# Starting every large on-chip tile of an encoder kernel at a multiple of 128 bytes

## The chip, the cores and the metric

The kernel runs on one core of a Trainium2 chip. The core has a matrix engine (TensorE, PE in the profile; its weight loads are listed apart as PEld), VectorE (DVE), ScalarE (ACT), GpSimd (POOL) and the engine that issues most transfers (SyncE, SP). They work side by side and wait for each other through semaphores. On-chip memory (SBUF) has 128 partitions; a tile takes the same stretch of bytes in each of them, and "place" below means the byte at which that stretch starts. The metric is the time of one execution in microseconds (us), lower is better.

## The reference

A two-layer encoder over 256 tokens of width 1024, float32:

```python
for i in range(2):
    hn = rms_norm(h, mix_norm[i])
    h = h + (retention_mixer(hn, ...) if i == 0 else fourier_mixer(hn, ...))
    hn = rms_norm(h, ffn_norm[i])
    h = h + (swiglu(hn, dense...) if i == 0 else moe_swiglu(hn, ...))   # 8 experts, top 2
return rms_norm(h, final_norm)

def swiglu(t, w_gate, w_up, w_down):
    return (jax.nn.silu(t @ w_gate) * (t @ w_up)) @ w_down
```

The retention mixer is four projections, rotary turns, a masked score product per head and an output product. The Fourier mixer is two small transform products and an output product. The expert layer (MoE) has 8 experts with a hidden width of 3584, so nearly all weights, and nearly all of the time, are there.

## The kernel before

Every large product is done in three matmuls per block, because each float32 operand is split in two rounded parts: `hi` and `lo = x - hi`. The weights come from memory in pieces of 1 MB (tile `raw`, issued by SP, up to 11 and for a while 15 buffers). ScalarE rounds a piece into `whi` (L103), VectorE subtracts it into `wlo` (L104), and TensorE uses the two parts. `whi` and `wlo` have three buffers each, in a pool of their own (`hilo`). The three matmuls are written in one helper, whose line numbers the profile shows:

```python
def mm3(o, lh, ll, rh, rl, first, last):
    te.matmul(o, lh, rh, start=first, stop=False)   # L225
    te.matmul(o, lh, rl, start=False, stop=False)   # L226
    te.matmul(o, ll, rh, start=False, stop=last)    # L227
```

The first operand (`lh` or `ll`, 128 columns of 4 bytes, so 512 bytes in a partition) is loaded into the array by a weight load, LDWEIGHTS in PEld. The second (`rh` or `rl`, 512 columns, so 2048 bytes) then streams through it. The profile writes a matmul as output<-streamed,loaded: `mm<-whi,xe` streams a piece of the weights through a loaded block of `xe`. So the model's weights are what streams, and the activations are what is loaded: every matmul loads another block of 512 bytes.

The loaded tiles by stage, in order of time:

- Retention (0 to about 230 us): `nhi`, `nlo` (the normalised input, transposed) for the projections; tiles named `th` (transposed queries, keys and gated outputs) for the scores and the output product; `ah`, `al` for the product of scores and values, where `vh`, `vl` stream.
- Dense layer (to about 402 us): `nhi`, `nlo` again, and `hth`, `htl` (the transposed hidden block) for the down product.
- Fourier stage (to about 450 us): `tsh`, `tsl` and `fh`, `fl` stream, `nhi` and `tdh`, `tdl` are loaded; then `yh`, `yl` are loaded for the output product.
- MoE (to the end): 56 units (8 experts by 7 blocks) of 48 matmuls that load `xe` and 24 that load `hth`, `htl`, with four transposes of the hidden block `hm` in each unit. For the last unit the transposed block is called `ht` and lies where `nhi` and `nlo` lay.

Order and waits come from the program text: `manual_schedule` keeps each engine's instructions as written. The places come from the tile pools. A pool lays its tiles one behind the other in the order in which their names first occur, each rounded up to 32 bytes, and a pool opened inside another begins behind it. Two small tiles of 32 bytes, `neg` and `iota8`, stand early in the pool `const`, so that all that follows in `const` starts 64 bytes past a multiple of 128. The pools of the stages (`pa`, `pb`, `pc`, `pe`, and `pt` at the right end) have such small tiles too.

Of the kernel before, what the change touches and what calls it, by code (L numbers as in the profile page):

```python
# [9 lines left out]
DT = mybir.dt  # L10
F32, F32R, BF, I32, U32 = DT.float32, DT.float32r, DT.bfloat16, DT.int32, DT.uint32
AF = mybir.ActivationFunctionType
OP = mybir.AluOpType
PS = bass.MemoryType.PSUM

P = 128
# [5 lines left out]
NE = 8  # L22
# [4 lines left out]
def cp(c):  # L27
    return slice(c * P, (c + 1) * P)
# [7 lines left out]
def cols(w, c0, n, k0, nk):  # L36

    return w.rearrange("(k p) n -> p k n", p=P)[:, k0:k0 + nk, c0:c0 + n]


class Weights:
# [82 lines left out]

def body(nc, tc, a, out, upto=None):
    with ExitStack() as ctx:
        const = ctx.enter_context(tc.tile_pool(name="const", bufs=1))
        r1 = ctx.enter_context(tc.tile_pool(name="r1", bufs=4))
        hilo = ctx.enter_context(tc.tile_pool(name="hilo", bufs=Weights.PARTS))
        ps = ctx.enter_context(tc.tile_pool(name="ps", bufs=1, space=PS))  # L130
# [66 lines left out]
        W.open(r1, 3, bufs=4)  # L197
        ident = const.tile([P, P], F32, name="ident")
        make_identity(nc, ident)
        neg = const.tile([P, 2], F32, name="neg")  # L200
        ge.memset(neg, -0.5)
        iota8 = const.tile([P, NE], F32, name="iota8")
        slot = const.tile([P, P], F32, name="slot")
        ones = const.tile([P, P], F32, name="ones")

        def route_consts(rw, upper):
            nc.scalar.dma_start(rw, a["moe_router"][0].rearrange("(k p) e -> p k e", p=P))
            kw = dict(base=0, allow_small_or_imprecise_dtypes=True)
            ge.iota(iota8, pattern=[[1, NE]], channel_multiplier=0, **kw)
            ge.iota(slot, pattern=[[1, P]], channel_multiplier=0, **kw)  # L210
            ge.memset(ones, 1.0)
            ge.iota(upper, pattern=[[1, P]], channel_multiplier=-1, **kw)
            ge.tensor_scalar(upper, upper, 0.0, None, op0=OP.is_gt)

        def acc(i):
            return ps.tile([P, 512], F32, name=f"acc{i}", tag=f"acc{i}")
# [32 lines left out]
        def scratch(pool):  # L249

            scr[:] = [pool.tile([P, 512], BF, name="scr")]
# [22 lines left out]
        def norm_tiles(pat, **kw):  # L274

            return [const.tile([P, 2048], F32R, name=n).rearrange(pat, **kw) for n in ("nhi", "nlo")]
# [43 lines left out]


        xh, xl = norm_tiles("p (k t) -> p k t", k=8)
        with tc.tile_pool(name="pa", bufs=1) as pa:
            scratch(pa)
            lx = pa.tile([P, 8], F32, name="lx")
            nc.scalar.dma_start(lx, bcast_rows(a["ret_decay_logit"][0], 8))
# [247 lines left out]

        H1 = P + 1
        pt_ = ctx.enter_context(ExitStack())
        pt = pt_.enter_context(tc.tile_pool(name="pt", bufs=1, side="right"))
        td = [pt.tile([P, 2, 512], F32R, name=n) for n in ("tdh", "tdl")]
        ts_ = [pt.tile([P, 2, 2 * H1], F32R, name=n) for n in ("tsh", "tsl")]
        rw = pt.tile([P, 8, NE], F32, name="rw")  # L580
        upper = pt.tile([P, P], F32, name="upper")
        with tc.tile_pool(name="pb", bufs=1) as pb:
            scratch(pb)
            tabr = pb.tile([P, 2, 2 * H1], F32, name="tabr")
            tabd = pb.tile([P, 2, 512], F32, name="tabd", tag="hth", bufs=2)
            accs = [acc(i) for i in range(4)]
            rst, sq = [], sq_tile()

            def dense_h(u, hooks={}):

                n, ns = (512, 2) if u < 5 else (256, 1)
                kn = 8 // ns
                o = []
                for s in range(ns):
                    wh, wl = W.get()
                    for c in range(2):
                        if not s:
                            o.append(mm())
                        for k in range(kn):
                            mm3(o[c][:, :n], xh[:, kn * s + k, cp(c)], xl[:, kn * s + k, cp(c)], wh[:, k], wl[:, k],  # L600
                                s == 0 and k == 0, s == ns - 1 and k == kn - 1)
                        run(hooks, 2 * s + c)
                return [x[:, :n] for x in o]

            def hidden(u):

                n = 4 if u < 5 else 2
                hT[u] = [pb.tile([P, 4, S], F32R, name=nm, bufs=2) for nm in ("hth", "htl")]
                return [lambda c=c: t4(hms[u][c], *(t[:, :n, cp(c)] for t in hT[u]), n) for c in range(2)]

            hms, hT = {}, {}
            for u in range(6):
                if u:
                    f = hidden(u - 1)
                    hooks = {0: f[:1], 1: f[1:]}
                else:
                    hooks = {1: [left]}
                n = 512 if u < 5 else 256
                g = dense_h(u, hooks)
                if not u:  # L620
                    for c in range(2):
                        for hf in range(2):
                            square(sq, c, hf)
                    rst = [inv_rms(sq, c) for c in range(2)]
                    nc.scalar.dma_start(tabr, a["dft_s"].rearrange("(c p) n -> p c n", p=P))
                    nc.scalar.dma_start(tabd, a["dft_d"].rearrange("(c p) n -> p c n", p=P))
                    gain_bcast(a["mix_norm"][1])
                    route_consts(rw, upper)
                gs = []
                for c in range(2):  # L630
                    t = pb.tile([P, 512], F32, name="gs", bufs=3)
                    se.activation(t[:, :n], g[c], AF.Silu, scale=rst[c])
                    gs.append(t)
                o = dense_h(u)
                if u == 1:
                    split(td[0], td[1], tabd)
                hms[u] = []
                for c in range(2):
                    t = pb.tile([P, 512], F32, name="hm", bufs=3)
                    ve.scalar_tensor_tensor(t[:, :n], o[c], rst[c], gs[c][:, :n], op0=OP.mult, op1=OP.mult)  # L640
                    hms[u].append(t)
                if 1 <= u < 5:
                    for s in range(2):
                        it = W.get()
                        for c in range(2):
                            out_mm(accs, it, *lhs(hT[u - 1], s), c, u == 1 and s == 0, False)
            it, f = W.get(), hidden(5)
            for c in range(2):
                out_mm(accs, it, *lhs(hT[4], 0), c, False, False)
                f[c]()  # L650
            its = [(W.get(), *lhs(hT[4], 1)), (W.get(hold=1), *lhs(hT[5], 0))]
            nh, nl = norm_tiles("p (c d) -> p c d", c=2)
            sq = sq_tile()

            rst = []

            def n_early(c, hf):
                square(sq, c, hf)
                if hf:
                    rst.append(inv_rms(sq, c))  # L660

            def n_sink(c, hf, xg):
                split(nh[:, c, HALF[hf]], nl[:, c, HALF[hf]], xg)
                if hf:
                    split_s(ts_[0][:, c], ts_[1][:, c], tabr[:, c], rst[c])
            left = close(its, accs, n_sink, n_early)
            left()
# [3 lines left out]


        with tc.tile_pool(name="pc", bufs=1) as pc:
            scratch(pc)
            gain_bcast(a["ffn_norm"][1])
            fq, yt = {}, {}
# [5 lines left out]
            def s1_out(o, g, b):  # L682

                if g % 2 == 0 and b == 0:
                    fq[g // 2] = [pc.tile([P, 2, 2, 2, H1], F32R, name=n, bufs=2) for n in ("fh", "fl")]
                h, l = fq[g // 2]
                split(h[:, b, :, g % 2], l[:, b, :, g % 2], o[:, :2 * H1].rearrange("p (w s) -> p w s", w=2))
# [28 lines left out]
            for c in range(2):  # L716
                for o, (g, b) in zip(early, gb8):
                    s1_mm(o, g, b, c)
                    if c:
                        s1_out(o, g, b)  # L720
            for p in range(2):
                stage2(p)
            accs = [acc(i) for i in range(4)]
# [80 lines left out]


        with tc.tile_pool(name="pe", bufs=1) as pe:
            def choose(e0):

                pm = pe.tile([P, 2, 2 * P], F32R, name="pm")
                for c in range(2):  # L810
                    for j in range(2):
                        ve.tensor_scalar(pm[:, c, cp(j)], slot, pos[:, c, e0 + j:e0 + j + 1],
                                         mask[:, c, e0 + j:e0 + j + 1], op0=OP.is_equal, op1=OP.mult)
                return pm
# [271 lines left out]
            for c in range(2):  # L1086
                x = [X[:, c, HALF[hf]] for hf in range(2)]
                se.activation(x[0], x[0], AF.Copy, scale=rs[c])  # L1088
                nc.scalar.dma_start(out[0, cp(c), HALF[0]], x[0])
                ve.scalar_tensor_tensor(x[1], of[c][1], rs[c], gb[:, HALF[1]], op0=OP.mult, op1=OP.mult)  # L1090
                nc.sync.dma_start(out[0, cp(c), HALF[1]], x[1])


NAMES = ["x", "mix_norm", "ffn_norm", "ret_w_in", "ret_decay_logit", "ret_gn_gain", "ret_w_out",
# [43 lines left out]
```

## Time and profile before

| | |
|---|---|
| median of 3 runs | 1451.75 us (1451.16 to 1452.35) |
| the profiled execution | 1451.45 us |
| its span, first to last instruction | 1449.6 us |
| PE busy in the span | 1430.3 us (99%) |
| DVE, ACT, POOL busy | 1184.3, 970.3, 61.5 us (82%, 67%, 4%) |
| granted TensorE clock, mean | 0.996 of full speed |
| moved by transfers | 431.70 MB, 298 GB/s on average |

A matmul's listed duration overlaps the next one's, so durations of one engine do not add up to its time. What adds up is the distance from one matmul's start to the next one's start, which is called the pace below.

### The profile page before, as it was taken

Reading aid. Unit: us, or ns where it says so; the run is one execution under the profiler, and the core shown is the slowest. Engines: PE = TensorE matmul, PEld = TensorE weight load, DVE = VectorE, ACT = ScalarE, POOL = GpSimd, SP = SyncE. Lnnn points to the kernel's source line nnn. Section 1 sums busy time; section 2 is a strip of 40 time slices with the busy share of each in tenths; the row PEclk is TensorE's granted clock in tenths of the full one; section 3 lists DMA queues with packets and bytes.
Section 4 is the critical chain, followed back from the end, with each engine's and each line's share of the span. In section 5 each row is a group of like instructions: output and inputs, shape, how many; then the busy total and the mean of one; then the engine's idle time right before and its main releaser. Section 6 shows DMA issues by size and latency. Waiting matters only on the chain. (4 is left out here: it accounts for less than half of the span.)

```text
span 1449.6 us, 17454 instructions
## 1 busy us (share of the span) xinstructions
PE 1430.3 (99%) x6603; PEld 1177.6 (81%) x6603; DVE 1184.3 (82%) x1236; ACT 970.3 (67%) x1123; POOL 61.5 (4%) x95
## 2 busy tenths in 40 slices
PE   8999999999999999999999999999999999999997
PEld 6888878888888888888888888888878888888886
DVE  6866666554577999989999998998989899999996
ACT  5544445443455777777877777777777777777875
POOL 8400000000001000000000000000000000000000
PEclk9999999999999999999999999999999999999999
DMA  7645549755526989999999999999999999999980
GB/s 285 211 151 200 170 139 362 247 183 175 198 103 239 382 311 362 348 336 345 347 357 372 376 348 334 368 365 352 338 388 341 342 360 379 352 378 375 348 317 29
DMA packets 185101, 431.70 MB, mean 298 GB/s; under 512 B 7977, under 2 KB 10801, under 8 KB 185010
## 3 DMA queue, kind: packets, MB, share of 16 engines
q1 hardware_dynamic: 181424, 426.27, 81.7%
q10 hardware_dynamic: 3586, 4.24, 0.9%
q8 instruction: 54, 0.88, 0.2%
q14 instruction: 37, 0.30, 0.1%
HBM read 429.44 MB, written 1.05 MB: 297 GB/s over the span
## 5 line engine op out<-in xcount | busy, mean ns | idle before, releaser
L104 DVE TENSOR_TENSOR wlo<-raw,whi 128x1024 fp32r<-128x1024 f32 (+1 forms) x789 | 923.4, 1218 | 146.4 <-ACT whi L103 140.4
L103 ACT CAST whi<-raw 128x1024 fp32r<-128x1024 f32 (+1 forms) x789 | 785.6, 1046 | 206.9 <-PE acc L227 105.7
L225 PE MATMUL mm<-whi,xe 128*128 128x512 f32 x896 | 355.3, 397 | 0.3 <-PEq L1064 0.3
L227 PE MATMUL mm<-whi,xe 128*128 128x512 f32 x896 | 350.0, 391 | 0.0
L226 PE MATMUL mm<-wlo,xe 128*128 128x512 f32 x896 | 349.1, 390 | 0.0
L226 PE MATMUL acc<-wlo,hth 128*128 128x512 f32 x528 | 208.2, 394 | 0.0
L225 PE MATMUL acc<-whi,hth 128*128 128x512 f32 x528 | 207.6, 393 | 0.0
L227 PE MATMUL acc<-whi,htl 128*128 128x512 f32 x528 | 205.6, 389 | 0.0
L227 PEld LDWEIGHTS mm<-whi,xe 128*128 128x128 f32 x896 | 168.2, 188 | 36.3
L225 PEld LDWEIGHTS mm<-whi,xe 128*128 128x128 f32 x896 | 168.3, 188 | 35.1 <-issue 2.2
L226 PEld LDWEIGHTS mm<-wlo,xe 128*128 128x128 f32 x896 | 168.5, 188 | 32.9
L225 PE MATMUL mm<-whi,nhi 128*128 128x512 f32 (+1 forms) x352 | 137.2, 390 | 0.0
L226 PE MATMUL mm<-wlo,nhi 128*128 128x512 f32 (+1 forms) x352 | 135.3, 384 | 0.0
L227 PE MATMUL mm<-whi,nlo 128*128 128x512 f32 (+1 forms) x352 | 135.3, 384 | 0.0
L225 PEld LDWEIGHTS acc<-whi,hth 128*128 128x128 f32 x528 | 99.1, 188 | 22.9
L227 PEld LDWEIGHTS acc<-whi,htl 128*128 128x128 f32 x528 | 99.1, 188 | 22.5
L226 PEld LDWEIGHTS acc<-wlo,hth 128*128 128x128 f32 x528 | 99.3, 188 | 20.2
L230 ACT CAST hth<-tr 128x512 fp32r<-128x512 f32 (+1 forms) x67 | 38.9, 581 | 91.1 <-PE tr L271 91.1
L227 PEld LDWEIGHTS mm<-whi,nlo 128*128 128x128 f32 x352 | 66.2, 188 | 14.6
L226 PEld LDWEIGHTS mm<-wlo,nhi 128*128 128x128 f32 x352 | 66.2, 188 | 13.5
L225 PEld LDWEIGHTS mm<-whi,nhi 128*128 128x128 f32 x352 | 66.2, 188 | 13.5
L231 DVE TENSOR_TENSOR htl<-tr,hth 128x512 fp32r<-128x512 f32 (+1 forms) x67 | 45.7, 681 | 33.8 <-ACT hth L230 33.7
(279 smaller groups left out, 1038.7 us busy)
## 6 DMA issues: line engine op xcount, KB each, us to landing
raw<-in_moe_w_gate SPq DMA_DIRECT2D x110, 1024.0 KB, 7.0
raw<-in_moe_w_down SPq DMA_DIRECT2D x108, 1024.0 KB, 7.1
raw<-in_moe_w_up SPq DMA_DIRECT2D x105, 1024.0 KB, 6.9
raw<-in_ret_w_in SPq DMA_DIRECT2D x23, 1024.0 KB, 5.2
raw<-in_dense_w_gate SPq DMA_DIRECT2D x11, 1024.0 KB, 5.2
raw<-in_dense_w_up SPq DMA_DIRECT2D x11, 1024.0 KB, 8.6
raw<-in_dense_w_down SPq DMA_DIRECT2D x11, 1024.0 KB, 5.4
raw<-in_ret_w_out SPq DMA_DIRECT2D x8, 1024.0 KB, 4.8
```

The source lines that it names most:

```text
L103: self.nc.scalar.copy(hi[sl], t[sl])
L104: self.nc.vector.tensor_sub(lo[sl], t[sl], hi[sl].bitcast(F32))
L225: te.matmul(o, lh, rh, start=first, stop=False)
L226: te.matmul(o, lh, rl, start=False, stop=False)
L227: te.matmul(o, ll, rh, start=False, stop=last)
L230: se.copy(hi, src)
L231: ve.tensor_sub(lo, src, hi.bitcast(F32))
```

## The change

A class `Aligned` is put around the pools `const`, `pa`, `pb`, `pc`, `pe` and `pt`. When a name occurs for the first time and its tile has 512 bytes or more in a partition, the class first takes a gap tile that nothing uses, so that the tile starts at a multiple of 128 bytes. `neg` and `iota8` move behind `nhi` and `nlo`. `upper` loses its own tile: it takes that of `tsh` after the first transform product, and is made there instead of in `route_consts`. No instruction is added or taken away, and no shape changes.

```diff
+class Aligned:
+    ALIGN = 128
+    def tile(self, shape, dtype, name, tag=None, bufs=1):
+        kw = dict(name=name, bufs=bufs, **({"tag": tag} if tag else {}))
+        size = math.prod(shape[1:]) * DT.size(dtype)
+        key = tag or name
+        if key not in self.seen:
+            self.seen.add(key)
+            gap = -self.at % self.ALIGN if size >= 512 else 0
+            if gap:
+                self.pool.tile([P, gap // 4], F32, name=f"gap{len(self.seen)}")
+            self.at += gap + bufs * (-(-size // 32) * 32)
+        return self.pool.tile(shape, dtype, **kw)
...
-        const = ctx.enter_context(tc.tile_pool(name="const", bufs=1))
+        const = Aligned(ctx.enter_context(tc.tile_pool(name="const", bufs=1)))
...
-        neg = const.tile([P, 2], F32, name="neg")
-        ge.memset(neg, -0.5)
-        iota8 = const.tile([P, NE], F32, name="iota8")
...
         xh, xl = norm_tiles("p (k t) -> p k t", k=8)
+        neg = const.tile([P, 2], F32, name="neg")
+        ge.memset(neg, -0.5)
+        iota8 = const.tile([P, NE], F32, name="iota8")
...
-        upper = pt.tile([P, P], F32, name="upper")
+        pt.fill(96)
...
-            ge.iota(upper, pattern=[[1, P]], channel_multiplier=-1, **kw)
-            ge.tensor_scalar(upper, upper, 0.0, None, op0=OP.is_gt)
...
+            upper = pt.tile([P, P], F32, name="upper", tag="tsh")
+            ge.iota(upper, pattern=[[1, P]], base=0, channel_multiplier=-1, allow_small_or_imprecise_dtypes=True)
+            ge.tensor_scalar(upper, upper, 0.0, None, op0=OP.is_gt)
             for p in range(2):
                 stage2(p)
```

Where the tiles lie in the two built programs, as the remainder of their place by 128, 256 and 512 (all slices of these tiles that a matmul loads or streams start at multiples of 512 bytes inside the tile, so they share these remainders; `whi`, `wlo`, `raw`, `xe`, `pm`, `y`, the placing tile `pt` of the MoE and `X` are where they were):

| tile | before: 128, 256, 512 | after: 128, 256, 512 |
|---|---|---|
| `whi`, `wlo` (streamed) | 0, 128, 128 | the same |
| `xe` | 0, 128, 128 | the same |
| `nhi`, `nlo`, `ht` | 64, 192, 192 | 0, 128, 128 |
| `th` of queries and keys, and of heads 1 and 3 | 96, 96, 352 | 0, 128, 128 |
| `th` of heads 0 and 2 | 32, 32, 32 | 0, 128, 384 |
| `ah`, `al` (with `vh`, `vl` streamed) | 64, 192, 192 (96, 96, 352) | 0, 128, 384 (0, 128, 128) |
| `hth`, `htl` of the dense layer | 32, 160, 160 | 0, 0, 256 |
| `yh`, `yl` | 0, 0, 256 | 0, 128, 384 |
| `hth`, `htl` of the MoE | 64, 64, 320 | 0, 128, 384 |
| `hm` of the MoE | 64, 64, 320 | 0, 128, 384 |

Only POOL's order changes. Its instructions from the end of the retention stage to the routing stage, before: `rs` is an inverse root of a norm, `slot`, `ones` and `upper` are constants of the routing, `w` are the routing weights.

```order
L264 TENSOR_TENSOR rs<-rs,neg 128x1 x2
L209 IOTA iota_90 128x8
L210 IOTA slot 128x128
L211 MEMSET ones 128x128
L212 IOTA upper 128x128
L213 TENSOR_SCALAR upper<-upper 128x128
L264 TENSOR_TENSOR rs<-rs,neg 128x1 x2
L759 MEMSET w 128x2
L760 TENSOR_TENSOR w<-sq 128x2
```

The same stretch of POOL after the change:

```order
L286 TENSOR_TENSOR rs<-rs,neg 128x1 x2
L233 IOTA iota_94 128x8
L234 IOTA slot 128x128
L235 MEMSET ones 128x128
L286 TENSOR_TENSOR rs<-rs,neg 128x1 x2
L750 IOTA upper 128x128
L751 TENSOR_SCALAR upper<-upper 128x128
L790 MEMSET w 128x2
L791 TENSOR_TENSOR w<-sq 128x2
```

The two instructions that make `upper` have moved behind the two roots of the dense layer's end; the first of them now waits for the matmuls that read `tsh`. The rows of the other engines are the same in both programs but for line and buffer numbers.

## Rows read from the trace of the kernel before

**Rows 1.** The page, busy time of each engine (us, share of the span, instructions).
```profile
PE 1430.3 (99%) x6603; PEld 1177.6 (81%) x6603; DVE 1184.3 (82%) x1236; ACT 970.3 (67%) x1123; POOL 61.5 (4%) x95
```

**Rows 2.** Waits of PE, first and last of nine: us, times, longest us.
```profile
PE tr L375 <- DMA X<-in_x: 2.3, 1, 2.3
...
PE mm L225 <- PEq L1064: 0.3, 1, 0.3
```

**Rows 3.** Busy time by window; the column names are the first line.
```profile
core 0: us, PE busy (x) PEld busy (x) DVE busy (x) ACT busy (x) POOL busy (x), PEclk, DMA share, GB/s
450.00:1400.00 950.00, 947.41 (x4335) 782.97 (x4335) 867.03 (x849) 727.65 (x798) 5.21 (x17) 1.00 0.98 356
```

**Rows 4.** Groups of PE instructions, MoE (470 to 1449 us): busy us, mean ns.
```profile
L226 PE MATMUL mm<-wlo,xe 128*128 128x512 f32 x883 | 344.0, 390 | 0.0
...
L226 PE MATMUL acc<-wlo,hth 128*128 128x512 f32 x440 | 173.4, 394 | 0.0
```

**Rows 5.** The same view before the MoE (0 to 450 us).
```profile
L226 PE MATMUL mm<-wlo,nhi 128*128 128x512 f32 x320 | 126.4, 395 | 0.0
...
L226 PE MATMUL acc<-wlo,hth 128*128 128x512 f32 x88 | 34.8, 396 | 0.0
...
L226 PE MATMUL acc<-wlo,th 128*128 128x512 f32 x64 | 25.3, 395 | 0.0
...
L226 PE MATMUL acc<-wlo,yh 128*128 128x512 f32 x32 | 12.6, 395 | 0.0
```

**Rows 6.** Timeline of PE (start us, duration us), `xe`, 21 matmuls apart.
```profile
898.40 0.39 PE L225 MATMUL mm<-whi,xe 128*128 128x512 f32 x1
...
903.16 0.39 PE L225 MATMUL mm<-whi,xe 128*128 128x512 f32 x1
```

**Rows 7.** Timeline of PE, `hth` of the MoE, 18 matmuls apart.
```profile
903.84 0.39 PE L225 MATMUL acc<-whi,hth 128*128 128x512 f32 x1
...
907.96 0.39 PE L225 MATMUL acc<-whi,hth 128*128 128x512 f32 x1
```

**Rows 8.** Timeline of PE, `ht` of the last unit, 18 matmuls apart.
```profile
1434.70 0.39 PE L225 MATMUL acc<-whi,ht 128*128 128x512 f32 x1
...
1438.90 0.39 PE L225 MATMUL acc<-whi,ht 128*128 128x512 f32 x1
```

**Rows 9.** Timeline of PE, `nhi` in the retention stage, 60 matmuls apart.
```profile
60.41 0.40 PE L225 MATMUL mm<-whi,nhi 128*128 128x512 f32 x1
...
74.41 0.40 PE L225 MATMUL mm<-whi,nhi 128*128 128x512 f32 x1
```

**Rows 10.** Timeline of PE, `yh` in the Fourier stage, 21 matmuls apart.
```profile
430.63 0.39 PE L226 MATMUL acc<-wlo,yh 128*128 128x512 f32 x1
...
435.53 0.40 PE L226 MATMUL acc<-wlo,yh 128*128 128x512 f32 x1
```

**Rows 11.** Groups of weight loads, whole run: busy us, mean ns, idle before.
```profile
L226 PEld LDWEIGHTS mm<-wlo,xe 128*128 128x128 f32 x896 | 168.5, 188 | 32.9
...
L226 PEld LDWEIGHTS mm<-wlo,nhi 128*128 128x128 f32 x352 | 66.2, 188 | 13.5
```

**Rows 12.** Chain that ended last (start us, us): transposes of two units in a row.
```profile
1177.74 0.44 PE tr L271 x4
...
1194.61 0.44 PE tr L271 x4
```

**Rows 13.** Timeline of PE behind a unit's transposes, 11 matmuls apart.
```profile
1419.01 0.40 PE L226 MATMUL mm<-wlo,xe 128*128 128x512 f32 x1
...
1421.55 0.39 PE L225 MATMUL mm<-whi,xe 128*128 128x512 f32 x1
```

**Rows 14.** Waits of ACT (us, times, longest), and transfers (KB, us to landing).
```profile
ACT whi L103 <- PE acc L227: 110.1, 105, 3.6
...
raw<-in_moe_w_gate SPq DMA_DIRECT2D x110, 1024.0 KB, 7.0
```

**Rows 15.** Timelines of POOL and PE: `upper` is finished, and first read.
```profile
231.58 0.55 POOL L213 TENSOR_SCALAR upper<-upper 128x128 f32<-128x128 f32 x1
...
450.14 0.37 PE L793 MATMUL po<-mask,upper 128*128 128x8 f32 x2
```

More of the change, by code (lines that the diff above doesn't have):

```diff
@@ L38, in cols, with __init__, fill @@
     return w.rearrange("(k p) n -> p k n", p=P)[:, k0:k0 + nk, c0:c0 + n]
+class Aligned:
+    ALIGN = 128
+    def __init__(self, pool):
+        self.pool, self.at, self.seen = pool, 0, set()
+    def tile(self, shape, dtype, name, tag=None, bufs=1):
[9 more added lines that the diff above has]
+        return self.pool.tile(shape, dtype, **kw)
+    def fill(self, over=0):
+        gap = (over - self.at) % self.ALIGN
+        if gap:
+            self.pool.tile([P, gap // 4], F32, name="gap")
 class Weights:
@@ L199, in body, with route_consts @@
         make_identity(nc, ident)
-        neg = const.tile([P, 2], F32, name="neg")
-        ge.memset(neg, -0.5)
-        iota8 = const.tile([P, NE], F32, name="iota8")
         slot = const.tile([P, P], F32, name="slot")
         ones = const.tile([P, P], F32, name="ones")
-        def route_consts(rw, upper):
+        def route_consts(rw):
             nc.scalar.dma_start(rw, a["moe_router"][0].rearrange("(k p) e -> p k e", p=P))
@@ L322, in body @@
         xh, xl = norm_tiles("p (k t) -> p k t", k=8)
+        neg = const.tile([P, 2], F32, name="neg")
+        ge.memset(neg, -0.5)
+        iota8 = const.tile([P, NE], F32, name="iota8")
         with tc.tile_pool(name="pa", bufs=1) as pa:
+            pa = Aligned(pa)
             scratch(pa)
@@ L576, in body @@
         pt_ = ctx.enter_context(ExitStack())
-        pt = pt_.enter_context(tc.tile_pool(name="pt", bufs=1, side="right"))
+        pt = Aligned(pt_.enter_context(tc.tile_pool(name="pt", bufs=1, side="right")))
         td = [pt.tile([P, 2, 512], F32R, name=n) for n in ("tdh", "tdl")]
@@ L580, in body @@
         rw = pt.tile([P, 8, NE], F32, name="rw")
-        upper = pt.tile([P, P], F32, name="upper")
+        pt.fill(96)
         with tc.tile_pool(name="pb", bufs=1) as pb:
+            pb = Aligned(pb)
             scratch(pb)
@@ L627, in body @@
                     gain_bcast(a["mix_norm"][1])
-                    route_consts(rw, upper)
+                    route_consts(rw)
                 gs = []
@@ L673, in body @@
         with tc.tile_pool(name="pc", bufs=1) as pc:
+            pc = Aligned(pc)
             scratch(pc)
@@ L806, in body @@
         with tc.tile_pool(name="pe", bufs=1) as pe:
+            pe = Aligned(pe)
             def choose(e0):
@@ L1091, in body @@
                 nc.sync.dma_start(out[0, cp(c), HALF[1]], x[1])
+        const.fill()
 NAMES = ["x", "mix_norm", "ffn_norm", "ret_w_in", "ret_decay_logit", "ret_gn_gain", "ret_w_out",
```

## The prediction

> **What bounds the kernel now.** I read the page first: PE is busy for 99% of the span, DVE for 82%, ACT for 67% [rows 1]. Then the waits: PE waits nine times in the whole run, from 2.3 us down to 0.3 us, together 11.6 us [rows 2]. So nothing that another engine does is worth much, and an edit pays only if it shortens PE's own stream of matmuls. The page does not say what that stream costs, because listed durations overlap. So I went to the timeline of PE and divided the distance between two starts by the matmuls between them. [...]
>
> - `xe`: (903.16 - 898.40) / 21 = 226.7 ns [rows 6]
> - `hth` of the MoE: (907.96 - 903.84) / 18 = 228.9 ns [rows 7]
> - `ht`, last unit: (1438.90 - 1434.70) / 18 = 233.3 ns [rows 8]
> - `nhi`: (74.41 - 60.41) / 60 = 233.3 ns [rows 9]
> - `yh`: (435.53 - 430.63) / 21 = 233.3 ns [rows 10]
>
> The grouped rows say the same more coarsely: a matmul lasts 390 ns with `xe`, 394 ns in the `wlo` line of the MoE's `hth` [rows 4], 395 to 396 ns with `nhi`, `th`, `yh` and the dense layer's `hth` [rows 5]. The weight loads themselves last 188 ns with `xe` as with `nhi` [rows 11]. So there is a step of 6.6 ns in the pace that goes neither with the streamed tile nor with the length of the load.
>
> What does it go with? `ht` and `hth` are the cleanest pair: same helper, same shapes, same kind of data, same streamed buffers, and only the place of the loaded tile differs (remainder by 256: 192 against 64); the pace differs by 4.4 ns [rows 7, 8]. So the place matters. But a multiple of 128 cannot be the whole rule: `yh` lies on one (remainder 0 by 128) and runs at the slow pace [rows 10]. What sets `xe` apart from all others in the table of places is that it has the remainder of the streamed tile by 256, namely 128. I take this as the working rule: a loaded tile with the remainder of `whi` by 256 runs at 226.7 ns, others at up to 233.3 ns.
>
> **The change part by part.** It adds and removes no instruction; what moves is places. By the table, after the change `nhi`, `nlo`, `ht`, all `th`, `yh`, `yl`, `ah`, `al` and the MoE's `hth`, `htl` have remainder 128 by 256, as `whi` has. The dense layer's `hth` and `htl` go from 160 to 0, where `yh` is now.
>
> First the pace that can really be reached. Behind each unit's transposes the `xe` stream needs some time to come back: its next 11 matmuls take (1421.55 - 1419.01) / 11 = 230.9 ns each [rows 13]. Over a whole unit, the transposes start every 16.87 us and last 0.44 us [rows 12], so 72 matmuls take 16.43 us. Of these 24 load `hth`: 24 x 228.9 = 5.49 us. The 48 with `xe` have 10.94 us, 227.9 ns each. I use 227.9 for the early stages, which have transposes in their streams too.
>
> - `nhi`, `nlo` with 512 columns: three lines of 320 [rows 5] and, by the code, 96 in the first query projection and the first value projection: 1056 x (233.3 - 227.9) = 5.7 us. The 96 matmuls with 256 columns I leave at nothing, for want of a row at another place.
> - `th` three lines of 64, `yh` three of 32 [rows 5], `ht` 24 and the products of `ah` with `vh` 48 (by the code): 360 x 5.4 = 1.9 us.
> - MoE `hth`: three lines of 440 [rows 4], from 228.9 to 226.7; they follow `xe` matmuls that are already back at the fast pace, so I take the undisturbed figure: 1320 x 2.2 = 2.9 us.
> - Dense `hth`: three lines of 88 [rows 5]. Remainder 0 is that of `yh`, at the same 233.3: nothing. If a multiple of 128 were enough: 264 x 5.4 = 1.4 us.
> - Transposes of `hm` move too. What follows them may come back sooner or later: at once would save 56 x 11 x (230.9 - 226.7) = 2.6 us; I take nothing and keep 2.6 us for the range, downwards and upwards.
> - `upper`: an iota and a 0.55 us operation [rows 15] go from the dense layer to the Fourier stage, behind the reads of `tsh`. On POOL nothing is queued behind them but the routing weights, which come later than `upper`'s first reader at 450.14 us [rows 15]. The transform products, the last readers of `tsh`, are over before `yh` is used, thus before 430 us [rows 10]. Some 20 us of the Fourier output product hide 1 us: nothing. Without that cover it would cost the 0.55 us and its iota.
> - DVE, ACT and transfers: their rows touch the tiles that stay (`raw`, `whi`, `wlo`) or take turns off the path; nothing.
>
> Can the suppliers keep up? In the MoE window DVE is busy 867.03 of 950 us, 91%, and the transfers bring 356 GB/s [rows 3]. The MoE becomes 2.9 us shorter, 0.3%, so DVE stays under 92%. ACT waits 110.1 us for PE to free weight buffers, and a piece lands 7.0 us after its issue [rows 14], while with 11 buffers and 16.87 us for 6 pieces it is needed some 30 us after. So PE keeps the lead and its saving reaches the end.
>
> Sum: 5.7 + 1.9 + 2.9 = 10.5 us. The profiled execution took 1451.45 us, 0.3 us less than the median of 1451.75: 1440.95 against the one, **1441.2 us** against the other.
>
> [...]
>
> **The rivals.**
>
> *The place is not the cause (no change).* The early stages would be slow for a reason of their own, as they show 395 to 396 ns with the loaded tile at remainders 0, 32, 64 and 96 by 128 alike [rows 5], and the loads last 188 ns at both paces [rows 11]. Against it stands the pair [rows 7, 8], where only the place changes. Time: 1451.7 us. [...]
>
> *The period is 512, not 256.* `whi` and `xe` share remainder 128 by 512 as well. Then `nhi`, `ht` and the `th` at 128 gain, by the code 1056 + 24 + 96: 1176 x 5.4 = 6.4 us. The MoE's `hth` goes from 320 to 384, which no row shows. If it keeps 228.9 the time is 1445.4; if it goes to 233.3 it loses 1320 x 4.4 = 5.8 us and the time is 1451.2.
>
> *The MoE's `hth` loses its good place (slower).* At 228.9 ns it is between the two paces, and no row says why. If its place at 64 is a lucky one, and the early stages are slow wherever their tiles lie, as four different remainders suggest [rows 5], they stay at 233.3 and `hth`, moved by 64 bytes, falls to the same: 1451.75 + 5.8 = 1457.6 us. It decides against the change as soon as `hth` runs above 228.9 ns and `nhi` does not move.
>
> **How the numbers follow.** The working rule has 0.69. Within it the time goes from 1436.8 (with the 1.4 us of the dense layer, 2.6 us of quicker returns, and 0.4 us for the 256-column and transposing matmuls that I left at nothing) to 1446.7 (no gain on `hth`, and 2.6 us of slower returns). The period of 512 has 0.14: 0.11 near 1445.4, 0.03 near 1451.2. No change from places has 0.11, the slower case 0.06. The range 1436.5 to 1448.5 us holds the first and the larger part of the second, 0.80. A measurement of this kernel tells 0.2%, 2.9 us, from no change: faster 0.69 + 0.11 = 0.80, same 0.03 + 0.11 = 0.14, slower 0.06.
>
> **What the profile of the changed kernel would show.** If I am right, `nhi`, `th` and `yh` matmuls last 390 ns in the groups instead of 395, with starts 226.7 ns apart in long runs; the MoE's `hth` lines all last 389 to 390 ns; the dense `hth` still 396. A unit of the MoE takes 16.87 - 24 x 0.0022 = 16.82 us. The weight loads stay at 188 ns and PE's waits at about 12 us. If `nhi` gains and `hth` rises towards 395, the period is 512. If dense `hth` falls to 390, a multiple of 128 is enough and `yh` was slow for another reason. If all stay, the place was not the cause. The prediction would also be wrong if PE began to wait in the MoE, which the list of waits would show as waits for `whi` or `wlo`.

## The result, and the profile after

The changed kernel takes 1440.88 us (median of 4 runs, 1440.62 to 1441.36) against 1452.05 us of the kernel before beside it (4 runs, 1451.16 to 1452.61): a ratio of 0.9924 with a 95% interval of 0.9912 to 0.9936, about 11 us or 0.76% faster. The forecast was 1441.2 us. The profiled execution took 1440.99 us, its span is 1439.2 us, and the mean granted clock is 0.996, as before.

The page's line of busy times, which answers to [rows 1]:

```profile
PE 1419.8 (99%) x6603; PEld 1178.0 (82%) x6603; DVE 1184.3 (82%) x1236; ACT 971.0 (67%) x1123; POOL 61.4 (4%) x95
```

The counts are the same, and PE's busy time is smaller by 10.5 us; the other engines' moved by 0.7 us at most. The span is shorter by 10.4 us, so nothing took the saving back. That is seen from the other side in PE's waits (us, times, longest us; first and last of ten entries, together 11.7 us, where nine entries made 11.6 us in [rows 2]; in both lists one entry counts two waits):

```profile
PE g L393 <- DMA gx<-in_mix_norm: 2.3, 1, 2.3
...
PE tr L293 <- DVE qn L459: 0.2, 1, 0.2
```

Lines have moved: the three matmuls of `mm3` are now L247, L248 and L249, the transposes L293. Groups of PE instructions up to 450 us (busy us, mean ns of one | idle before), which answer to [rows 5]:

```profile
L248 PE MATMUL mm<-wlo,nhi 128*128 128x512 f32 x320 | 124.6, 390 | 0.0
...
L248 PE MATMUL acc<-wlo,hth 128*128 128x512 f32 x88 | 34.7, 394 | 0.0
...
L248 PE MATMUL acc<-wlo,th 128*128 128x512 f32 x64 | 25.0, 390 | 0.0
...
L248 PE MATMUL acc<-wlo,yh 128*128 128x512 f32 x32 | 12.5, 390 | 0.0
...
L248 PE MATMUL mm<-wlo,nhi 128*128 128x256 f32 x32 | 9.0, 282 | 0.0
```

The last of these lines is of matmuls with 256 columns. In the kernel before it was:

```profile
L226 PE MATMUL mm<-wlo,nhi 128*128 128x256 f32 x32 | 8.9, 278 | 0.0
```

And in the MoE, which answer to [rows 4]:

```profile
L248 PE MATMUL mm<-wlo,xe 128*128 128x512 f32 x873 | 340.2, 390 | 0.0
...
L248 PE MATMUL acc<-wlo,hth 128*128 128x512 f32 x440 | 171.2, 389 | 0.0
```

In these lines all 512-column matmuls whose loaded tile was moved to the remainder of `whi` by 256 now show 389 to 390 ns. The dense layer's `hth`, which went to 0, shows 394, near its old 396. The timeline of PE gives the paces behind these rounded means:

```profile
60.41 0.39 PE L247 MATMUL mm<-whi,nhi 128*128 128x512 f32 x1
...
74.01 0.39 PE L247 MATMUL mm<-whi,nhi 128*128 128x512 f32 x1
...
419.62 0.39 PE L247 MATMUL acc<-whi,yh 128*128 128x512 f32 x1
...
424.38 0.39 PE L247 MATMUL acc<-whi,yh 128*128 128x512 f32 x1
...
895.91 0.39 PE L249 MATMUL acc<-whi,htl 128*128 128x512 f32 x1
...
899.99 0.39 PE L249 MATMUL acc<-whi,htl 128*128 128x512 f32 x1
...
1168.97 0.40 PE L248 MATMUL mm<-wlo,xe 128*128 128x512 f32 x1
...
1171.51 0.39 PE L247 MATMUL mm<-whi,xe 128*128 128x512 f32 x1
```

- `nhi`, 60 matmuls apart: (74.01 - 60.41) / 60 = 226.7 ns, in [rows 9] 233.3.
- `yh`, 21 apart: (424.38 - 419.62) / 21 = 226.7 ns, in [rows 10] 233.3.
- `htl` of the MoE, 18 apart: (899.99 - 895.91) / 18 = 226.7 ns, in [rows 7] 228.9.
- `xe` behind the transposes, 11 apart: (1171.51 - 1168.97) / 11 = 230.9 ns, the same as in [rows 13].

Two units in a row, in the chain that ended last: their transposes start 16.81 us apart, where [rows 12] has 16.87 and the forecast was 16.82.

```profile
1304.70 0.44 PE tr L293 x4
...
1321.51 0.44 PE tr L293 x4
```

Where did the 10.4 us come from? The start of the last `yl` matmul moved from 445.93 to 438.90 us, so 7.0 us come from before the MoE. From the first to the last `xe` matmul it took 1426.76 - 459.42 = 967.34 us and now 1416.50 - 452.56 = 963.94 us: 3.4 us. The stretch between the two, routing, took 0.2 us more, the tail 0.1 us less.

### The profile page after: what moved, and what is told of

It reads as the page before. It is cut to its first block, busy times and chain, and to the rows that moved or that the text cites. A ratio compares the mean times of both kernels' runs of the same rounds, so it can differ in the third digit from the quotient of the medians.

```text
span 1439.2 us, 17455 instructions
## 1 busy us (share of the span) xinstructions
PE 1419.8 (99%) x6603; PEld 1178.0 (82%) x6603; DVE 1184.3 (82%) x1236; ACT 971.0 (67%) x1123; POOL 61.4 (4%) x95
## 5 line engine op out<-in xcount | busy, mean ns | idle before, releaser
L247 PE MATMUL mm<-whi,xe 128*128 128x512 f32 x896 | 355.0, 396 | 0.3 <-PEq L1096 0.3
L249 PE MATMUL mm<-whi,xe 128*128 128x512 f32 x896 | 349.6, 390 | 0.0
L248 PE MATMUL mm<-wlo,xe 128*128 128x512 f32 x896 | 349.2, 390 | 0.0
L247 PE MATMUL acc<-whi,hth 128*128 128x512 f32 x528 | 206.2, 390 | 0.0
L249 PE MATMUL acc<-whi,htl 128*128 128x512 f32 x528 | 205.9, 390 | 0.0
L248 PE MATMUL acc<-wlo,hth 128*128 128x512 f32 x528 | 205.9, 390 | 0.0
L249 PEld LDWEIGHTS mm<-whi,xe 128*128 128x128 f32 x896 | 168.2, 188 | 36.0
L247 PEld LDWEIGHTS mm<-whi,xe 128*128 128x128 f32 x896 | 168.3, 188 | 34.9 <-issue 2.2
L248 PEld LDWEIGHTS mm<-wlo,xe 128*128 128x128 f32 x896 | 168.6, 188 | 32.9
L247 PE MATMUL mm<-whi,nhi 128*128 128x512 f32 (+1 forms) x352 | 135.7, 386 | 0.0
L249 PE MATMUL mm<-whi,nlo 128*128 128x512 f32 (+1 forms) x352 | 133.9, 380 | 0.0
L248 PE MATMUL mm<-wlo,nhi 128*128 128x512 f32 (+1 forms) x352 | 133.7, 380 | 0.0
L249 PEld LDWEIGHTS acc<-whi,htl 128*128 128x128 f32 x528 | 99.1, 188 | 21.1
L247 PEld LDWEIGHTS acc<-whi,hth 128*128 128x128 f32 x528 | 99.2, 188 | 20.8
L248 PEld LDWEIGHTS acc<-wlo,hth 128*128 128x128 f32 x528 | 99.2, 188 | 20.8
L249 PEld LDWEIGHTS mm<-whi,nlo 128*128 128x128 f32 x352 | 66.2, 188 | 12.9
L248 PEld LDWEIGHTS mm<-wlo,nhi 128*128 128x128 f32 x352 | 66.3, 188 | 12.0
L247 PEld LDWEIGHTS mm<-whi,nhi 128*128 128x128 f32 x352 | 66.2, 188 | 11.8
```

## The experiments

Four theories were open. A: what counts is the distance of the loaded tile from the streamed one, by 256 bytes. B: the loaded tile's own place must be 128 by 256. C: any multiple of 128 is enough. D: the place is not the cause. A and B are the two readings of the prediction's working rule, which could not tell them apart, as `whi` never moved.

**The place by itself.** This kernel leaves the model out. 48 matmuls in a row (`hi`, `hi`, `lo` as in `mm3`) make a series, and from series to series only the places change:

```diff
+        mov[r] = place(r, 8192, f"mov{r}x", F32R)          # streamed, remainder r = 128, 0, 64
+        held[r] = t[:, :512]; held[r + 16] = t[:, 4:516]   # loaded, remainder r and r + 16
...
+        for r in range(0, 512, 16): wide(128, r)           # 512 columns
+        for r in range(0, 512, 64): wide(0, r)
+        for r in range(0, 512, 64): wide(64, r)
+        for r in range(0, 512, 32): narrow(128, r)         # 256 columns
```

> This kernel leaves the model out: it only streams matmuls in the pattern of the three-part product (load hi, hi, lo) and returns rows of x. Series of 48 matmuls: 32 series with the streamed tile at remainder 128 by 512 and the loaded tile at remainders 0, 16, ... 496, then 8 with the streamed tile at 0 and 8 with it at 64 (loaded 0, 64, ... 448), all with 512 columns, then 16 with 256 columns. Theory A (what counts is the distance of the loaded from the streamed tile by 256): with the streamed tile at 128, 226.7 ns at loaded 128 and 384 and about 233.3 ns at most others; with the streamed tile at 0 the fast places move to 0 and 256, with it at 64 to 64 and 320. Theory B (an absolute place, 128 by 256, is good): the fast places stay at 128 and 384 for every streamed tile. Theory C (a multiple of 128 is good): fast at 0, 128, 256 and 384. Theory D (the place is not the cause): the same pace in all series of 512 columns, 226.7 or 233.3 ns. For 256 columns the theories say nothing; in the two kernels the pace was about 113 ns at a distance of 64 and about 120 ns at 0.

The pace of a series is the time from its first matmul to the next series' first, divided by 48. The timeline of PE, first matmuls of neighbouring series (`held128x` serves the remainders 128 and 144, and so on):

```profile
97.95 0.39 PE L52 MATMUL mm<-mov128x,held128x 128*128 128x512 f32 x1
...
108.83 0.39 PE L52 MATMUL mm<-mov128x,held128x 128*128 128x512 f32 x1
...
364.68 0.39 PE L52 MATMUL mm<-mov0x,held0x 128*128 128x512 f32 x1
...
375.58 0.40 PE L52 MATMUL mm<-mov0x,held64x 128*128 128x512 f32 x1
...
386.77 0.39 PE L52 MATMUL mm<-mov0x,held128x 128*128 128x512 f32 x1
...
397.93 0.40 PE L52 MATMUL mm<-mov0x,held192x 128*128 128x512 f32 x1
```

Streamed at 128 and loaded at 128: (108.83 - 97.95) / 48 = 226.7 ns. Streamed at 0, loaded at 0: (375.58 - 364.68) / 48 = 227.1 ns, loaded at 128: (397.93 - 386.77) / 48 = 232.5 ns. All series with 512 columns, by distance (loaded less streamed, by 256), in ns; the first series of the program is left out, since its matmuls started up to 595 ns apart:

| distance | streamed at 128 | streamed at 0 | streamed at 64 |
|---|---|---|---|
| 0 | 226.7, 226.7 | 227.0, 227.1 | 226.9, 227.1 |
| 16 | 226.8, 226.9 | | |
| 32 to 112 | 231.8 to 234.2 | 233.3 (at 64) | 233.3 (at 64) |
| 128 | 233.4 | 232.5 | 232.5 |
| 144 | 226.9, 233.4 | | |
| 160, 176 | 233.4, 230.2, 233.2, 229.9 | | |
| 192 | 233.4, 229.0 | 229.1 | 229.3, 229.1 |
| 208, 224 | 233.2 to 233.3 | | |
| 240 | 227.1, 227.1 | | |

The good place goes with the streamed tile: 128, 0 and 64 by 256, each time distance 0, at 226.7 to 227.1 ns. So A holds here, with a period of 256; B, C and D do not, and neither does a period of 512, since loaded tiles at 128 and 384 give the same 226.7 ns. The short pace is not at distance 0 alone: 16 (226.8, 226.9 ns) and 240 (227.1 ns) have it too in this order. The table also names the kernel's odd figures. The MoE's `hth` before, at distance 192, ran at 228.9 [rows 7], `nhi` at distance 64 at 233.3 [rows 9], `yh` at distance 128 at 233.3 [rows 10]. What the table leaves open are the distances 144, with two paces 6.5 ns apart, and 192, with 233.4 ns once and 229.0 to 229.3 otherwise.

**The same in the opposite order.** Only the order of the first 32 series changes; the model is left out again.

```diff
-        for r in range(0, 512, 16):
+        for r in range(496, -1, -16):
             wide(128, r)
```

> The series of matmuls without the model once more, with the first 32 series in the opposite order: streamed tile at 128, loaded tile at 496, 480, ... 0. In the first order the distances (loaded less streamed, by 256) of 240, 0 and 16 gave 226.7 to 227.1 ns in both passes over the 256 bytes, but the distance 144 gave 226.9 ns in one pass and 233.4 in the other, and 192 gave 233.4 and 229.0. If the place alone sets the pace, each loaded place shows the pace that it had before. If the pace also hangs on what ran ahead, the distances between the extremes change with the order, while 240, 0 and 16 stay at 226.7 to 227.1 ns and 32 to 112 at 232 to 234.

```profile
247.77 0.40 PE L52 MATMUL mm<-mov128x,held160x 128*128 128x512 f32 x1
...
258.97 0.40 PE L52 MATMUL mm<-mov128x,held128x 128*128 128x512 f32 x1
...
270.17 0.39 PE L52 MATMUL mm<-mov128x,held128x 128*128 128x512 f32 x1
...
281.05 0.39 PE L52 MATMUL mm<-mov128x,held96x 128*128 128x512 f32 x1
```

The series at distance 16 begins at 258.97 us, that at 0 at 270.17 us. Distance 0 is back at (281.05 - 270.17) / 48 = 226.7 ns although a series at the long pace ran ahead. Distance 16 now takes (270.17 - 258.97) / 48 = 233.3 ns, where it took 226.8 behind a series at distance 0. So my expectation that 16 would keep its pace was wrong: behind a short pace it ran at 226.8 ns, in the opposite order at 233.3. 144 was at 233.2 in both passes of this order, 192 at 229.2, 240 at 226.9. Distances 0 and 240 gave 226.7 to 227.6 ns in every series of both orders, 240 in the first order behind series at 233.3 ns. The other distances showed a short and a long pace (16: 226.8 and 233.3 ns; 144: once 226.9, else 233.2 to 233.4) or stayed at 229 ns and more.

**Parts of the change in the kernel.** Three kernels apply it in pieces. Constants: only `neg` and `iota8` move behind `nhi`, which puts `nhi`, `nlo` and `ht` at 128 by 256. MoE: only the pool `pe` is aligned. Stages: only `pa`, `pb` and `pc`.

```diff
 # constants: no class Aligned; of the change only
         xh, xl = norm_tiles("p (k t) -> p k t", k=8)
+        neg = const.tile([P, 2], F32, name="neg")
+        ge.memset(neg, -0.5)
+        iota8 = const.tile([P, NE], F32, name="iota8")
 # MoE: of the change only
         with tc.tile_pool(name="pe", bufs=1) as pe:
+            pe = Aligned(pe)
 # stages: of the change only
+            pa = Aligned(pa)
+            pb = Aligned(pb)
+            pc = Aligned(pc)
```

> The kernel before with neg and iota8 moved behind nhi and nlo, and nothing else: only the tiles of the const pool change place (nhi, nlo and ht from 192 to 128 by 256). Theories A, B and C: nhi and ht gain 1080 x 5.4 = 5.8 us, less some 0.5 us that the matmuls of 256 columns lose: about 1446.7 against 1452.0. MoE hth stays at 228.9, th and yh at 233.3 ns. Theory D: 1452.0.

> The kernel before with the aligning class on the MoE's pool alone: hth and htl go from 64 to 128 by 256 (384 by 512), hm with them. Theories A, B and C: 1320 x 2.2 = 2.9 us, about 1449.1 against 1452.0, with hth at 226.7 and all early stages at 233.3 ns. A period of 512 would leave hth at 228.9 or worse. Theory D: 1452.0.

> The kernel before with the aligning class on the pools of the retention, dense and Fourier stages: th, ah, yh go to 128 by 256, dense hth from 160 to 0. Theories A and B: th, yh and ah gain 336 x 5.4 = 1.8 us, dense hth nothing: about 1450.2. Theory C: dense hth gains 1.4 us more: 1448.8. Theory D: 1452.0.

The kernel before took 1451.7 us on that chip (median of 20 runs, 1450.84 to 1452.57).

| part | median, us (runs) | ratio, 95% interval | gain, us |
|---|---|---|---|
| constants | 1446.48 (1446.05 to 1446.79) | 0.9964, 0.995 to 0.9978 | 5.2 |
| MoE | 1447.73 (1447.08 to 1449.02) | 0.9975, 0.9966 to 0.9985 | 4.0 |
| stages | 1449.66 (1449.2 to 1450.52) | 0.9986, 0.9977 to 0.9995 | 2.0 |

The three add up to 11.2 us, as much as the whole change gained (1452.05 - 1440.88); each gain has an interval of 1 to 2 us to either side, so the agreement to a tenth is luck. The pool `pt` and `upper`, which the whole change moves as well, are in none of the three. Each part moves the mean paces of its own groups, by 3 to 6 ns (`hth` of the MoE by 2.3, the dense layer's by 1), and no other group of 512 columns by more than about 1 ns: with the MoE's pool alone, the group of `wlo` with `hth` in the MoE shows 389 ns, and that with `nhi` up to 450 us still 395.

```profile
L253 PE MATMUL mm<-wlo,nhi 128*128 128x512 f32 x320 | 126.4, 395 | 0.0
...
L253 PE MATMUL acc<-wlo,hth 128*128 128x512 f32 x440 | 171.2, 389 | 0.0
```

The MoE's part gives 4.0 us where 2.9 were expected. From its first to its last `xe` matmul this kernel takes 1422.76 - 459.11 = 963.65 us, 3.7 less than the 967.34 of before. 1320 `hth` matmuls from 228.96 to 226.69 ns are 3.0 us of it. The other 0.7 us lies in the `xe` matmuls, which did not move: their mean pace falls from 227.98 to 227.72 ns (the gaps between starts below 300 ns), times 2688. Most of it, 0.55 us, is in the nine matmuls behind each unit's transposes (from the second start to the eleventh), which take 2075 instead of 2085 ns. In the two other kernels of this group `xe` stays at 227.97 and 227.94 ns. Whether the new place of `hm` or that of `hth` does this, these three kernels do not tell; the next group does.

**The rule put to use, and against itself.** Four kernels on one chip: the changed kernel again; one with the dense layer's `hth` at distance 0 too; one in which everything but the tiles at the right end of the memory lies 128 bytes lower, so that their places change and the distances among them stay; and one that then puts 128 bytes back in front of `whi`, so that `nhi` is a multiple of 128 but at distance 128.

```diff
 # dense layer at distance 0
-            pb = Aligned(pb)
+            pb = Aligned(pb, 256)
 # all lower
-    nc = bacc.Bacc("TRN2", target_bir_lowering=False, num_devices=1, dynamic_dma_scratch_size=1024)
+    nc = bacc.Bacc("TRN2", target_bir_lowering=False, num_devices=1, dynamic_dma_scratch_size=896)
 # constants lower: as above, and
         hilo = ctx.enter_context(tc.tile_pool(name="hilo", bufs=Weights.PARTS))
+        hilo.tile([P, 32], F32, name="gaph", bufs=1)
```

> The changed kernel itself once more, beside the other kernels of this job. Every theory expects 1440.9 us, 10.8 us below the kernel before.

> The changed kernel, but the pool of the dense layer starts its tiles at multiples of 256, so that its hth and htl go from remainder 0 to 128 by 256, the remainder of whi; nothing else that a matmul loads moves by this. Theory A (what counts is the distance of the loaded tile from the streamed one by 256): 264 matmuls go from 232.4 to about 227.5 ns, 1.3 us less, 1439.6 us, and the dense hth lines show 390 ns where the changed kernel shows 394 to 397. Theory C (a multiple of 128 is enough) and theory D (the place is not the cause): 1440.9 us, and 394 to 397 ns as there.

> The changed kernel with 128 bytes less of DMA scratch at the bottom of the memory, so that every tile but those at its right end lies 128 bytes lower: whi, xe, nhi, th, yh and the MoE's hth all go from remainder 128 to 0 by 256, and all distances between streamed and loaded tiles stay. Theory A (distance): 1440.9 us and the same paces. Theory B (the loaded tile's own place must be 128 by 256): everything falls to 233.3 ns, so 2688 matmuls with xe lose 5.6 ns each, 1320 with hth 6.6, and 1416 of the early stages 5.6: 15 + 9 + 8 = 32 us, less 1.4 for the dense hth which would gain: about 1471 us. Theory C (a multiple of 128): 1440.9 us.

> As the kernel in which everything lies 128 bytes lower, but with 128 bytes put back in front of whi, so that only the pools ahead of whi stay lower: nhi, nlo, ht (loaded), X, raw (first four), ident and gx are at remainder 0 by 256 and whi and all loaded tiles of the stages at 128, as in the changed kernel. Distance of nhi from whi: 128. Theory A (distance by 256): the 1056 matmuls with nhi lose 5.6 ns each, 5.9 us, 1446.8 us, and their lines show 395 ns. Theory C (a multiple of 128 is enough, for nhi is on one): 1440.9 us and 390 ns. Theory B: 1446.8 us too.

The kernel before took 1451.23 us here (10 runs, 1450.6 to 1453.39).

| kernel | median, us (runs) | ratio, 95% interval |
|---|---|---|
| changed, again | 1440.63 (1440.47 to 1441.92) | 0.9924, 0.991 to 0.9938 |
| dense layer at distance 0 | 1439.96 (1439.83 to 1440.57) | 0.992, 0.9907 to 0.9934 |
| all lower | 1441.79 (1440.27 to 1441.91) | 0.993, 0.9916 to 0.9943 |
| constants lower | 1446.79 (1446.34 to 1447.68) | 0.9967, 0.9955 to 0.9979 |

*All lower* lies in the range of the changed kernel again, not 30 us above it, though `whi`, `xe`, `nhi` and `hth` are all at 0 by 256. Its groups up to 450 us, and in the MoE:

```profile
L248 PE MATMUL mm<-wlo,nhi 128*128 128x512 f32 x320 | 124.6, 389 | 0.0
...
L248 PE MATMUL mm<-wlo,xe 128*128 128x512 f32 x873 | 340.2, 390 | 0.0
L248 PE MATMUL acc<-wlo,hth 128*128 128x512 f32 x440 | 171.2, 389 | 0.0
```

That is the end of theory B in the kernel. *Constants lower* loses 6.2 us against the changed kernel again, with `nhi` on a multiple of 128; that is the end of theory C. 5.9 us were expected. Its groups show `nhi` back at 395 ns while `hth` of the MoE keeps 389:

```profile
L249 PE MATMUL mm<-wlo,nhi 128*128 128x512 f32 x320 | 126.3, 395 | 0.0
...
L249 PE MATMUL acc<-wlo,hth 128*128 128x512 f32 x440 | 171.2, 389 | 0.0
```

*Dense layer at distance 0* is the quickest median of all, 0.7 us under the changed kernel, but with so small a step single runs of the two overlap. The trace is clearer: the last `htl` matmul of the dense layer starts at 400.24 us, and at 401.37 us in the changed kernel beside it, 1.1 us earlier where 1.3 were expected, and the group shows it:

```profile
L248 PE MATMUL acc<-wlo,hth 128*128 128x512 f32 x88 | 34.3, 389 | 0.0
```

*What the quicker return behind the transposes goes with.* A transpose loads a block of `hm` and streams `ident`, the identity matrix: the trace of the changed kernel lists it as `tr<-ident,hm`, 272 ns on average in the MoE. `ident` lies in `const` ahead of all that was moved, at 128 by 256 in the kernel before and in the changed one, so `hm` went from distance 192 to 0 from it. In *constants lower* the MoE's `hth`, `hm`, `xe` and `whi` lie as in the changed kernel; of the tiles that TensorE reads in a unit (but for the last unit's `ht`) only `ident` lies 128 bytes lower, which puts `hm` at distance 128 from it. There the nine matmuls behind the transposes take 2084 ns and the mean pace of `xe` is 227.95 ns, as before the change, although `hth` has its new place. In all nine kernels the two figures go with the distance of `hm` from `ident`: 2075 to 2076 ns and 227.7 ns at distance 0 (five kernels), 2083 to 2085 ns and 227.9 to 228.0 ns at 192 (three), 2084 ns and 227.95 ns at 128 (this one). So in these kernels it goes not with the place of `hth`, but with that of the two tiles of the transposes to each other; how they reach the matmuls behind them is not shown.

## Why the prediction was right

- *PE's stream is the bound, so its shortening reaches the end.* Right: PE busy fell by 10.5 us, the span by 10.4 us, and the waits went from 11.6 to 11.7 us. The suppliers kept up: no wait for `whi` or `wlo` is on the list.
- *A loaded tile with the remainder of `whi` by 256 runs at 226.7 ns.* Right, and the series show the reason for its form: it is the distance to the streamed tile. The rule had been read from one tile, `xe`; that the early stages followed it was the step with the greatest risk, as their four remainders by 128 all looked alike [rows 5]. All of them were at distances that show a long pace without the model too: `nhi` at 64 and the dense `hth` at 32 (231.8 to 234.2 ns from 32 to 112), `yh` at 128 (232.5 to 233.4), `th` at 160 (233.2 and 233.4) and 224 (233.2 to 233.3).
- *`nhi`, `nlo`: 5.7 us, with 227.9 ns as the pace that can be reached.* The constants alone gained 5.2 us. The mean pace came to 227.7 ns.
- *`th`, `yh`, `ah`: 1.9 us with `ht`.* The stages alone gained 2.0 us.
- *MoE `hth`: 2.9 us.* 3.0 us, by the pace.
- *`hm` and the return behind the transposes: nothing, bound 2.6 us.* It gave 0.7 us, the largest term that I had missed; it goes with the distance of `hm` from `ident`, which the prediction did not look at.
- *Dense `hth`: nothing.* Nearly: 233.3 to 232.4 ns times 264 is 0.2 us.
- *The 96 matmuls with 256 columns: nothing.* They became slower, 278 to 282 ns in the `wlo` line and on average 116.6 to 121.3 ns apart, 0.5 us lost. The prediction had no row for them and put them at nothing.
- *`upper`: nothing.* Right: it is finished at 409.98 us and first read at 443.10 us.
- *The sum, 10.5 us.* The medians differ by 11.2 us, the profiled spans by 10.4. The terms left at nothing came to +0.7, +0.2 and -0.5 us, and that they nearly cancel is luck. The three terms of the sum themselves came out within 0.5 us each.
- *Rivals.* A period of 512 is excluded by the series, and by `hth` of the MoE, which gained at remainder 384. That the place is not the cause is excluded by the series and by each of the three parts. That `hth` would lose a lucky place did not happen: at 228.9 ns it was between the two paces, as the distance 192 is without the model (229.0 to 229.3 ns, once 233.4).

With the same streamed tile the pace without the model is 226.7 or 233.4 ns by the place of the loaded one, at distances 0 and 128. The runs show that it goes with the distance; why it does is not shown.

## What to carry to other kernels

Where PE hardly ever waits (here 11.6 us in a span of 1449.6), compare the pace, start to start, of matmuls that differ only in which tile is loaded; a step between equal shapes may come from their places. Lay the loaded tiles at the streamed tile's remainder by 256 bytes: with 512 columns this was worth up to 6.6 ns in 233 here, while a multiple of 128 alone gave all of it (`nhi`, 233.3 to 226.7 ns, at distance 0 from `whi`) or nearly nothing (the dense `hth`, 233.3 to 232.4 ns, at distance 128). With 256 columns it lost 0.5 us here (see also the next section). Moving everything but the tiles at the right end together by 128 bytes changed nothing that the runs show (1441.79 us, 1440.27 to 1441.91, against 1440.63, 1440.47 to 1441.92), so one gap in front of a pool may be enough.

## What the runs showed that I had not expected

- At two distances the series showed a short and a long pace. At distance 16 a series ran at 226.8 ns behind a short pace and at 233.3 behind a long one; at distance 144 it showed 226.9, 233.4 and twice 233.2. Only at distances 0 (226.7 ns) and 240 (227.1 ns) is a short pace seen right behind a series at 233.3 ns. Each of the two orders was run once. Why two distances side by side differ so is open.
- With 256 columns the order of the places is another one: 113.9 and 117.9 ns at distance 64, 118.6 at 128, 117.8 and 117.7 at 192, but 120.0 and 119.8 at distance 0, where 512 columns ran at 226.7 ns, their shortest. These series ran in one order only, with the streamed tile at 128.
- The loads themselves last 188 ns at either pace: with `nhi` in [rows 11], at 233.3 ns, and in the changed kernel, at 226.7 ns. What changes is when the next matmul starts, and a matmul's listed duration, 395 and 390 ns in the `wlo` line.
